# Matmuls of 256 columns in place of one of 512 in most k steps, and operand tiles at multiples of 2048 bytes

## The chip, the cores and the metric

The kernel runs on one core of one Trainium2 chip. The metric is the device time of one execution in microseconds (us); lower is better. A core has a matrix engine (PE, whose weight loads the profile lists apart as PEld), a vector engine (DVE), a scalar engine (ACT), GpSimd (POOL) and a sync engine (SP), which here issues nearly all transfers.

## The reference

One layer of an encoder trunk on 256 tokens with D = 2048, all in float32:

```python
u = rms_norm(h, norm_mix); proj = u @ w_in                      # 2048 x 5200
h = h + concat(gated_deltanet(...), mla_attention(...)) @ w_out
h = h + memory_cross_attention(rms_norm(h, norm_xattn), mem_n, wq, wk, wv, wo)
h = h + conv_ffn(rms_norm(h, norm_ffn), w_up, conv_w, conv_b, w_down)   # D_FF = 5632
return rms_norm(h, norm_final)
```

Nearly all arithmetic is in the products of 256 tokens with w_in, w_out, the four matrices of the cross-attention, w_up and w_down.

## The kernel before

**Products in three parts.** Each float32 operand is split into a high part, rounded to the matrix engine's one-pass format (fp32r), and the rest. A product is the sum of three: high weight by high token, high weight by low token, low weight by high token. A token tile `x(k)` holds, for 128 of the features, 256 columns of high parts and behind them 256 of low parts: 512 columns, 2048 bytes in each partition.

**k steps and output blocks.** Weights stay in the array, tokens move. One output block is 128 output features by 256 tokens in a PSUM tile `psg` of 512 columns. It is summed over k steps of 128 input features: 16 for a 2048-wide input, 44 for w_down, 8 for half a block of w_out. `kstep` (line 115) does one step with two matmuls: `wh` against all 512 columns (line 122, high result in columns 0 to 255, low in 256 to 511), and `wl` against the 256 high columns (line 120). `turn_` makes every other step take `wl` first, so that two products of one width stand side by side. `halves` and `add_res` add the two halves of the PSUM tile when they take it out. `kstep3` (lines 125 to 127) does the same step as three matmuls of 256 columns, all into columns 0 to 255; it is used where the result has no second half to add: `q_block` (tiles `xq`), the `lath` products, the scores (`kh`, `qh`), the mix of values (`pTx`, `vh`) and the last block of w_down. `v_block` (lines 958 to 960) has the tokens as weights and moves 512 columns of `wh` or `wl`.

**Weights.** `load_w` brings 128 x 1024 float32 (eight k steps) into `raw` by SP's queue; `split_w` makes `wh` on ACT (line 102) and `wl` on DVE (line 103). All three have four buffers in `wpool`.

**Order on PE.** The matrix engine's order is the order in which the code is written. Up to the cross-attention a queue of k steps (`drawn`, `enqueue`) is drawn by `fill(n)` between the small matmuls of attention and delta rule, so that PE has work while ACT and DVE prepare those. After that the blocks simply follow each other; `rstd_col` and `rstd_row` put a few small matmuls for a norm between two of them.

**Where the tiles lie.** Pools are laid out one behind the other in the order in which the program opens them. A tile's place in a partition, as the program was built:

| tile | first byte | modulo 2048 |
|---|---|---|
| `raw`, `wh`, `wl` (4 buffers each, 4096 bytes) | 19776, 36160, 52544 | 1344 |
| `small` pool, 10432 bytes | 68928 | 1344 |
| token tiles `u`, `xq`, `fx`, `xo`, `mh`, `om`, `od`, `ga` (16384 bytes a half) | 79360 and every 16384 on | 1536 |
| `gb`, feed-forward | 161280 | 1536 |
| `kh`, `qh`, `pTx`, `vh` | 204288, 194048, 214528, 218624 | 1536 |

One k step's weights are 512 bytes of `wh` or `wl`, so they begin at 1344, 1856, 320 or 832 modulo 2048. A moving operand begins at 1536 (high, or all 512 columns) or 512 (low).

Of the kernel before, what the change touches and what calls it, by code (L numbers as in the profile page):

```python
# [9 lines left out]
F32 = mybir.dt.float32  # L10
# [11 lines left out]
P = 128  # L22
T = 256
# [47 lines left out]
def trunk(ctx, tc, a):  # L71
    nc = tc.nc
    V, S, PE = nc.vector, nc.scalar, nc.tensor

    const = ctx.enter_context(tc.tile_pool(name="const", bufs=1))
    wpool = ctx.enter_context(tc.tile_pool(name="wpool", bufs=4))
    small = ctx.enter_context(tc.tile_pool(name="small", bufs=2))
    abpool = ctx.enter_context(tc.tile_pool(name="abpool", bufs=4))
    pg = ctx.enter_context(tc.tile_pool(name="pg", bufs=3, space=PSUM))
    pa = ctx.enter_context(tc.tile_pool(name="pa", bufs=5, space=PSUM))  # L80
# [1 line left out]
    def psg():  # L82
        return pg.tile([P, 512], F32, name="psg", tag="psg")

    def psa(tag="a"):
        return pa.tile([P, 512], F32, name="ps" + tag, tag=tag, bufs=1 if tag == "c" else 2)
# [19 lines left out]
    def load_w(src, n=1024, pieces=1):  # L106
        raw = wpool.tile([P, 1024], F32, name="raw", tag="raw")
        nc.sync.dma_start(raw[:, 0:n], src)
        return split_w(raw, n, pieces)

    turn_ = [False]

    def kstep(ps, wh, wl, xh2, first, last):
        rev = turn_[0] and not first
        turn_[0] = not rev
        for lo in ((True, False) if rev else (False, True)):
            if lo:
                PE.matmul(ps[:, 0:256], wl, xh2[:, 0:256], start=False, stop=last, skip_group_check=True)  # L120
            else:
                PE.matmul(ps[:, 0:512], wh, xh2, start=first, stop=last, skip_group_check=True)  # L122

    def kstep3(ps, wh, wl, xh2, first, last):
        PE.matmul(ps[:, 0:T], wh, xh2[:, 0:T], start=first, stop=False)  # L125
# [3 lines left out]
    def gemm_block(w, nb, x, step=kstep):  # L129
        ps = psg()  # L130
        for hf in range(2):
            wh, wl = load_w(w[2 * nb + hf])
            for j in range(8):
                k = 8 * hf + j
                step(ps, wh[:, j * P:(j + 1) * P], wl[:, j * P:(j + 1) * P], x(k), k == 0, k == KC - 1)
        return ps
# [22 lines left out]

    cg = const.tile([P, NCG], F32, name="cg")  # L160
    sm = const.tile([P, NSM], F32, name="sm")
    eps = const.tile([P, 1], F32, name="eps")
    epq = const.tile([P, 1], F32, name="epq")
    ones = cg[:, K_ONE:K_ONE + P]
# [1 line left out]


    def rstd_col(*accs):
        ps = psa("c")
        for t in range(2):  # L170
            for i, acc in enumerate(accs):
                PE.matmul(ps[:, t:t + 1], acc[:, t * P:(t + 1) * P], ones[:, 0:1], start=i == 0,
                          stop=i == len(accs) - 1)
        r = small.tile([P, 2], F32, name="rcol", tag="rcol", bufs=2)
        S.activation(r, ps[:, 0:2], AF.Sqrt, scale=1.0 / D, bias=eps)
        V.reciprocal(r, r)
        return r

    def rstd_row(col):
        ps = psa("c")  # L180
        for t in range(2):
            PE.matmul(ps[:, t * P:(t + 1) * P], col[:, t:t + 1].to_broadcast([P, P]), idn, start=True, stop=True)
        r = small.tile([P, T], F32, name="rrow", tag="rstd", bufs=2)
        S.copy(r, ps[:, 0:T])
        return r
# [4 lines left out]
    with ExitStack() as ph:  # L190
# [11 lines left out]
        with tc.tile_pool(name="xpool", bufs=1) as xpl:  # L202
# [13 lines left out]
            for k in range(KC):  # L216
                wh, wl = w0[k // 8]
                j = k % 8
                kstep(ps0, wh[:, j * P:(j + 1) * P], wl[:, j * P:(j + 1) * P], u(k), k == 0, k == KC - 1)
# [49 lines left out]
        def drawn():  # L269
            ready = {0: lead}  # L270
            ps = None
            i = 0
            while i < len(queue):
                for n in range(i, min(i + 1 + ahead[0], len(queue))):
                    if n not in ready:
                        ready[n] = load_w(queue[n][0], pieces=2)
                _, x, begin, first, last, done = queue[i]
                if begin:
                    begin()
                wh, wl = ready.pop(i)  # L280
                if first:
                    ps = psg()
                for j in range(8):
                    kstep(ps, wh[:, j * P:(j + 1) * P], wl[:, j * P:(j + 1) * P], x(j),
                          first and j == 0, last and j == 7)
                    if last and j == 7:
                        done(ps)
                    pos[0] += 1
                    for at_, f in [t for t in later if t[0] <= pos[0]]:
                        later.remove((at_, f))  # L290
                        f()
                    yield
                i += 1
# [3 lines left out]
        gen = drawn()  # L297

        def fill(n):
            for _ in range(n):  # L300
                next(gen, None)

        def until(n):
            fill(n - pos[0])
# [66 lines left out]
        with ExitStack() as ms:  # L371
# [20 lines left out]

            lats.append(latent)
            fill(8)
            rs0 = rstd_col(*accs)
            fill(6)
            rs.append(rstd_row(rs0))
            latent(0, ps0)
            latent(1, ps1)
            until(Q0 + 8)  # L400
            ps = psa()
# [72 lines left out]
            ps = psa()  # L474
# [5 lines left out]
            ps = psa()  # L480
# [22 lines left out]
            def w_mla(i):  # L503
                c = order.index(i)
                for n in order[c:c + 2]:
                    if n not in wm:
                        wm[n] = load_w(a["w_mla"][n])
                return wm[i]
# [63 lines left out]
            for i in range(2):  # L572
                kn = mp.tile([P, 4, T], F32, name="kn", tag="kn")
                wh, wl = w_mla(i)
                for n in range(4):
                    ps = psg()
# [8 lines left out]
                wh, wl = w_mla(2 + i)  # L585
                for t in range(2):
                    ps = psg()
# [325 lines left out]
    with ExitStack() as ph:  # L913
# [4 lines left out]
        for n in range(KC):  # L918
            wh, wl = load_w(a["w_out"][2 * n + 1])
            ps = psg()  # L920
# [15 lines left out]
        for n in range(KC):  # L936
            ps = gemm_block(a["xa_wk"], n, mh)
            if n == 0:
                rmc = rstd_col(macc)
                psk = ps  # L940
            else:
                if n == 1:
                    rsm = rstd_row(rmc)
                    normed(psk, rsm, kT[:, 0])
                normed(ps, rsm, kT[:, n])
            split_gain(xq(n), hT[:, n], sm[:, C_XA + n:C_XA + n + 1])
            accum_sq(xacc, hT[:, n], n == 0)
# [80 lines left out]
        for n in range(3):  # L1028
            v_block(n)
            if n == 0:  # L1030
                rcx = rstd_col(xacc)
            elif n == 1:
                rsx = rstd_row(rcx)
# [23 lines left out]
        for n in range(KC):  # L1057
            if n < 3:
                ps = pw[n]
            else:  # L1060
                ps = psg()
# [10 lines left out]
    with ExitStack() as ph:  # L1072
# [39 lines left out]
        for n in range(KC):  # L1112
            ps = psg()
            for c in range(6):
                nk = 8 if c < 5 else 4
                o = n * NF * P + c * 1024
                wh, wl = load_w(a["w_down"][n, :, c * 1024:c * 1024 + nk * P], nk * P)
# [131 lines left out]
```

## Time and profile before

| | |
|---|---|
| three runs, median | 1580.1 us (1579.47 to 1580.53) |
| profiled execution | 1580.7 us |
| its span, first to last instruction | 1578.9 us |
| mean granted PE clock | 0.994 |
| PE busy | 1546.1 us, 98% |
| DVE, ACT, POOL busy | 1119.3, 889.3, 147.9 us |
| moved by DMA | 282.22 MB, 179 GB/s |

Starts of matmuls are recorded, their ends are modelled; so the pace of PE is read from the distance between two starts, and not from the duration of one. A busy share of 98% says that PE had a matmul under way, not that its columns came at full rate.

### The profile page before, as it was taken

How to read it: one execution, taken by the hardware profiler on the slowest of the kernel's cores; microseconds unless marked ns; L12 is line 12 of the kernel's file. 1: busy time of each engine (PE TensorE's matmuls, PEld its weight loads, DVE VectorE, ACT ScalarE, POOL GpSimd, SP SyncE). 2: the span in 40 equal slices, each digit the busy share in tenths (PEclk: the TensorE clock that was granted, in tenths of full speed). 3: DMA queues.
4: the chain of work that ended last, by engine and by line, in shares of the span. 5: the costliest groups of instructions: out<-in, count | busy, mean ns of one | idle time of the engine just before them, and what ended most of it. 6: DMA issues, size and time to landing. Idle time of an engine off the chain costs nothing.

```text
span 1578.9 us, 24577 instructions
## 1 busy us (share of the span) xinstructions
PE 1546.1 (98%) x9386; PEld 1358.5 (86%) x9386; DVE 1119.3 (71%) x1810; ACT 889.3 (56%) x1473; POOL 147.9 (9%) x152
## 2 busy tenths in 40 slices
PE   7999999999999999999999999999999999999996
PEld 5887877888888889999888888888888888888886
DVE  8687688696976555566777888878888886445453
ACT  7867666757764444455556666556665665344441
POOL 2224021001320000000110000000000000111112
PEclk9999999999999999999999999999999999999998
DMA  7564443364665555544555555555555556666663
GB/s 248 179 214 141 144 134 126 118 214 132 200 200 189 191 188 193 174 161 133 174 188 187 187 189 190 194 188 189 192 193 187 187 190 183 190 190 183 198 187 106
DMA packets 80773, 282.22 MB, mean 179 GB/s; under 512 B 9392, under 2 KB 10304, under 8 KB 80656
## 3 DMA queue, kind: packets, MB, share of 16 engines
q1 hardware_dynamic: 79344, 277.86, 54.3%
q0 software_dynamic: 1312, 2.80, 0.6%
q8 instruction: 73, 1.20, 0.3%
q14 instruction: 44, 0.36, 0.1%
HBM read 277.83 MB, written 2.11 MB: 177 GB/s over the span
## 4 chain that ended last, share of the span: by engine, by line
PE 88%; DVE 5%; ACT 4%; issue 1%; DMA 1%; SPq 0%; DVEq 0%; ACTq 0%
PE psg L122 46%; PE psg L120 23%; PE psg L125 3%; PE psg L126 3%; PE psg L127 3%; PE psg L960 2%; PE psg L959 2%; PE psg L958 2%; DVE wl L103 2%; ACT wh L102 1%; DMA raw<-in_w_out_dram 1%; PE psa L620 0%; PE psa L539 0%; DVE qkv L330 0%; DVE hT L1132 0%
## 5 line engine op out<-in xcount | busy, mean ns | idle before, releaser
L103 DVE TENSOR_TENSOR wl<-raw,wh 128x1024 fp32r<-128x1024 f32 (+2 forms) x614 | 647.3, 1061 | 286.1 <-ACT wh L102 279.2
L102 ACT CAST wh<-raw 128x1024 fp32r<-128x1024 f32 (+2 forms) x614 | 550.8, 909 | 401.5 <-PE psg L122 243.2
L122 PE MATMUL psg<-fx,wh 128*128 128x512 f32 x1408 | 439.8, 393 | 0.0
L120 PEld LDWEIGHTS psg<-fx,wl 128*128 128x128 f32 x1408 | 264.7, 188 | 60.0
L120 PE MATMUL psg<-fx,wl 128*128 128x256 f32 x1408 | 277.6, 279 | 0.0
L122 PE MATMUL psg<-u,wh 128*128 128x512 f32 x624 | 207.7, 404 | 8.9 <-DVE u L149 8.2
L122 PEld LDWEIGHTS psg<-fx,wh 128*128 128x128 f32 x1408 | 212.0, 188 | 0.0
L120 PEld LDWEIGHTS psg<-u,wl 128*128 128x128 f32 x624 | 119.3, 192 | 29.3 <-DVE wl L103 3.1
L140 ACT COPY half<-psg 128x256 f32<-128x256 f32 x143 | 53.2, 372 | 154.9 <-PE psg L122 154.7
L120 PE MATMUL psg<-u,wl 128*128 128x256 f32 x624 | 134.3, 289 | 1.7 <-DVE wl L103 1.7
L122 PE MATMUL psg<-gb,wh 128*128 128x512 f32 x420 | 133.4, 393 | 0.0
L122 PEld LDWEIGHTS psg<-u,wh 128*128 128x128 f32 x624 | 99.3, 191 | 12.5 <-DVE u L149 9.0
L120 PEld LDWEIGHTS psg<-gb,wl 128*128 128x128 f32 x420 | 79.0, 188 | 17.9
L1089 DVE SCALAR_TENSOR_TENSOR y<-ub,sm,y 128x256 f32<-128x256 f32 x176 | 84.7, 482 | 3.5 <-ACT y L1087 0.3
L120 PE MATMUL psg<-gb,wl 128*128 128x256 f32 x420 | 82.8, 278 | 0.0
L122 PE MATMUL psg<-mh,wh 128*128 128x512 f32 x256 | 80.5, 394 | 0.0
L122 PE MATMUL psg<-xo,wh 128*128 128x512 f32 x256 | 80.4, 393 | 0.0
L141 DVE TENSOR_TENSOR ub<-psg,half 128x256 f32<-128x256 f32 x88 | 37.4, 425 | 60.1 <-ACT half L140 60.1
L122 PE MATMUL psg<-ga,wh 128*128 128x512 f32 x240 | 77.3, 393 | 0.0
L125 PE MATMUL psg<-xq,wh 128*128 128x256 f32 x256 | 71.2, 278 | 0.0
L126 PE MATMUL psg<-xq,wh 128*128 128x256 f32 x256 | 70.9, 277 | 0.0
L127 PE MATMUL psg<-xq,wl 128*128 128x256 f32 x256 | 70.9, 277 | 0.0
(405 smaller groups left out, 2411.3 us busy)
## 6 DMA issues: line engine op xcount, KB each, us to landing
raw<-in_w_up_dram SPq DMA_DIRECT2D x176, 512.0 KB, 3.4
raw<-in_w_down_dram SPq DMA_DIRECT2D x80, 512.0 KB, 4.2
raw<-in_w_in_dram SPq DMA_DIRECT2D x77, 512.0 KB, 3.9
raw<-in_w_out_dram SPq DMA_DIRECT2D x32, 512.0 KB, 4.2
raw<-in_xa_wk_dram SPq DMA_DIRECT2D x32, 512.0 KB, 3.5
raw<-in_xa_wv_dram SPq DMA_DIRECT2D x32, 512.0 KB, 3.5
raw<-in_xa_wq_dram SPq DMA_DIRECT2D x32, 512.0 KB, 3.4
raw<-in_xa_wo_dram SPq DMA_DIRECT2D x32, 512.0 KB, 3.4
```

Source lines behind the costliest of these rows:

```text
L102: S.copy(wh[:, c], raw[:, c])
L103: V.tensor_sub(wl[:, c], raw[:, c], wh[:, c].bitcast(F32))
L120: PE.matmul(ps[:, 0:256], wl, xh2[:, 0:256], start=False, stop=last, skip_group_check=True)
L122: PE.matmul(ps[:, 0:512], wh, xh2, start=first, stop=last, skip_group_check=True)
L125: PE.matmul(ps[:, 0:T], wh, xh2[:, 0:T], start=first, stop=False)
L126: PE.matmul(ps[:, 0:T], wh, xh2[:, T:2 * T], start=False, stop=False)
L127: PE.matmul(ps[:, 0:T], wl, xh2[:, 0:T], start=False, stop=last)
L140: S.copy(t, ps[:, T:2 * T])
L141: V.tensor_add(out, ps[:, 0:T], t)
L958: PE.matmul(pss[t], xh, wh[:, wk], start=(k == 0), stop=False)
L959: PE.matmul(pss[t], xh, wl[:, wk], start=False, stop=False)
L1089: V.scalar_tensor_tensor(y, b[:, j:j + T], sm[:, cw + j:cw + j + 1], y, ALU.mult, ALU.add)
```

## The change

`kstep` takes one of two forms. If it is the first step of an output block, or if the flag `wide` is set, the high weights meet all 512 columns as before. In every other step the high weights meet the high and the low 256 columns in two matmuls, both into columns 0 to 255, and the low weights follow always; the order no longer turns. The flag is set at each call of `fill`, `rstd_col` and `rstd_row`, and cleared by every step. The pool `small` is opened ahead of `wpool`, and a constant of 512 bytes that nothing reads is put in: `wpool` then begins at 30720, the token tiles at 79872, `gb` at 161792, and each of these is a multiple of 2048. All other tiles behind them move by 512 bytes.

```diff
     const = ctx.enter_context(tc.tile_pool(name="const", bufs=1))
+    small = ctx.enter_context(tc.tile_pool(name="small", bufs=2))
     wpool = ctx.enter_context(tc.tile_pool(name="wpool", bufs=4))
-    small = ctx.enter_context(tc.tile_pool(name="small", bufs=2))
...
-    turn_ = [False]
+    wide = [True]
 
     def kstep(ps, wh, wl, xh2, first, last):
-        rev = turn_[0] and not first
-        turn_[0] = not rev
-        for lo in ((True, False) if rev else (False, True)):
-            if lo:
-                PE.matmul(ps[:, 0:256], wl, xh2[:, 0:256], start=False, stop=last, skip_group_check=True)
-            else:
-                PE.matmul(ps[:, 0:512], wh, xh2, start=first, stop=last, skip_group_check=True)
+        if first or wide[0]:
+            PE.matmul(ps[:, 0:512], wh, xh2, start=first, stop=last, skip_group_check=True)
+        else:
+            PE.matmul(ps[:, 0:T], wh, xh2[:, 0:T], start=False, stop=False, skip_group_check=True)
+            PE.matmul(ps[:, 0:T], wh, xh2[:, T:2 * T], start=False, stop=False, skip_group_check=True)
+        wide[0] = False
+        PE.matmul(ps[:, 0:T], wl, xh2[:, 0:T], start=False, stop=last, skip_group_check=True)
...
+    const.tile([P, 128], F32, name="pad")
...
     def rstd_col(*accs):
+        wide[0] = True
...
     def rstd_row(col):
+        wide[0] = True
...
         def fill(n):
+            wide[0] = True
             for _ in range(n):
                 next(gen, None)
```

## Rows read from the trace of the kernel before

**Rows 1.** The page: the engines' busy time, and granted clock in 40 slices.

```profile
PE 1546.1 (98%) x9386; PEld 1358.5 (86%) x9386; DVE 1119.3 (71%) x1810; ACT 889.3 (56%) x1473; POOL 147.9 (9%) x152
PEclk9999999999999999999999999999999999999998
```

**Rows 2.** Windows: stretch, length, busy time of each engine, granted clock, DMA share, GB/s.

```profile
0.00:100.00 100.00, 87.65 (x482) 74.59 (x483) 78.82 (x156) 75.57 (x156) 23.45 (x31) 0.98 0.64 215
200.00:300.00 100.00, 94.06 (x637) 80.11 (x636) 76.76 (x175) 65.17 (x143) 13.98 (x9) 0.97 0.37 124
1000.00:1100.00 100.00, 100.00 (x579) 87.68 (x578) 81.49 (x127) 60.33 (x91) 0.00 (x0) 1.00 0.57 190
```

**Rows 3.** Groups of PE instructions: the matmuls of line 122, count, busy and mean.

```profile
L122 PE MATMUL psg<-fx,wh 128*128 128x512 f32 x1408 | 439.8, 393 | 0.0
...
L122 PE MATMUL psg<-u,wh 128*128 128x512 f32 x624 | 207.7, 404 | 8.9 <-DVE u L149 8.2 <-ACT wh L102 0.6
...
L122 PE MATMUL psg<-gb,wh 128*128 128x512 f32 x420 | 133.4, 393 | 0.0
...
L122 PE MATMUL psg<-mh,wh 128*128 128x512 f32 x256 | 80.5, 394 | 0.0
L122 PE MATMUL psg<-xo,wh 128*128 128x512 f32 x256 | 80.4, 393 | 0.0
L122 PE MATMUL psg<-ga,wh 128*128 128x512 f32 x240 | 77.3, 393 | 0.0
...
L122 PE MATMUL psg<-om,wh 128*128 128x512 f32 x128 | 41.9, 398 | 0.0
L122 PE MATMUL psg<-od,wh 128*128 128x512 f32 x128 | 40.2, 394 | 0.4 <-DVE hT L875 0.4
```

**Rows 4.** Timeline of PE in w_up: start us, us, engine, line, tiles, shape, count.

```profile
1000.31 0.39 PE L120 MATMUL psg<-fx,wl 128*128 128x256 f32 x2
1000.54 0.62 PE L122 MATMUL psg<-fx,wh 128*128 128x512 f32 x2
...
1011.40 0.39 PE L120 MATMUL psg<-fx,wl 128*128 128x256 f32 x2
```

**Rows 5.** Timeline of PE and its weight loads in `q_block`.

```profile
607.46 0.28 PE L125 MATMUL psg<-xq,wh 128*128 128x256 f32 x1
607.57 0.28 PE L126 MATMUL psg<-xq,wh 128*128 128x256 f32 x1
607.58 0.19 PEld L127 LDWEIGHTS psg<-xq,wl 128*128 128x128 f32 x1
...
612.56 0.28 PE L125 MATMUL psg<-xq,wh 128*128 128x256 f32 x1
```

**Rows 6.** Timeline of PE: into and out of the last block of w_down.

```profile
1548.96 0.39 PE L122 MATMUL psg<-gb,wh 128*128 128x512 f32 x1
1549.19 0.28 PE L125 MATMUL psg<-ga,wh 128*128 128x256 f32 x1
...
1564.74 0.28 PE L172 MATMUL psc<-cg,oacc 128*128 128x1 f32 x2
```

**Rows 7.** Timeline of PE: from `v_block` into the scores and out of them.

```profile
650.28 0.39 PE L960 MATMUL psg<-wh,mh 128*128 128x512 f32 x1
...
650.63 0.28 PE L126 MATMUL psa<-kh,qh 128*128 128x256 f32 x1
...
653.27 0.28 PE L127 MATMUL psa<-kh,qh 128*128 128x256 f32 x1
653.39 0.28 PE L125 MATMUL psg<-xq,wh 128*128 128x256 f32 x1
```

**Rows 8.** Timeline of PE: from `q_block` into the mix of values.

```profile
675.71 0.28 PE L127 MATMUL psg<-xq,wl 128*128 128x256 f32 x1
...
675.94 0.28 PE L126 MATMUL psa<-pTx,vh 128*128 128x256 f32 x1
...
677.62 0.28 PE L125 MATMUL psa<-pTx,vh 128*128 128x256 f32 x1
```

**Rows 9.** Timeline of PE: `q_block` interrupted by four transposes.

```profile
659.05 0.60 PE L1007 MATMUL psc<-cg,sx 128*128 128x128 f32 x4
...
659.84 0.28 PE L125 MATMUL psg<-xq,wh 128*128 128x256 f32 x1
...
660.52 0.28 PE L125 MATMUL psg<-xq,wh 128*128 128x256 f32 x1
```

## Prediction

> **What bounds the kernel now.** I read the page's busy times first, then the windows, the groups of PE, and last the timeline of PE, start by start. PE is busy for 98% of the span and at its full clock in nearly every slice [rows 1]. The windows say where it is not: it idles 12.4 us in the first 100 us and 5.9 us between 200 and 300 us; in a stretch of w_up it never stops, while DVE has 18% and the DMA engines 43% to spare [rows 2]. So from about 400 us on only one thing can change the time: how far apart the starts of successive matmuls are.
>
> The unit to count in is the k step. `kstep` runs 3460 times, the sum of the eight groups of line 122 [rows 3]. In w_up, 16 pairs of steps lie between 1000.31 and 1011.40 us: 11.09 us by 32 steps is 346.6 ns a step [rows 4]. At 2.4 GHz, the upper of PE's two clock levels and the one granted here (1.00), its 768 columns would pass in 320 ns.
>
> The timeline also shows what three matmuls of 256 columns cost, and that is the surprise of this trace: they have three prices, although columns, shape and granted clock are the same.
>
> - In `q_block`, 15 steps from 607.46 to 612.56 us: 340.0 ns a step, 113.3 ns a matmul [rows 5].
> - In the last block of w_down, 44 steps from 1549.19 to 1564.74 us: 353.4 ns a step, 117.8 ns a matmul [rows 6].
> - In the scores, 22 matmuls from 650.63 to 653.27 us, and in the mix of values, 14 from 675.94 to 677.62 us: 120.0 ns each, so 360.0 ns a step [rows 7, 8].
>
> The present step stands in the middle of the three. The sign of the change is therefore the question which price the new steps get.
>
> **What sets the price.** Waiting does not: these stretches run without a gap. The weight load of the next matmul starts 0.01 us after the matmul itself [rows 5], so a load of weights and a stream of tokens read SBUF side by side all the time, and both are nearly as long as the distance of two starts. Two things differ between the streams.
>
> One is where the two operands lie. In `q_block` and the last block, weights begin at 1344 plus a multiple of 512 and tokens at 1536 or 512: 320 apart modulo 512. In the scores and in the mix both begin at 1536 plus multiples of 512: 0 apart. Every stream with distance 0 runs at 120.0 ns, whatever went before: a 512-column stream in the scores [rows 7], the quick 113.3 ns stream in the mix [rows 8]. It takes the slow price from its second matmul on. I take the distance as the cause, though these streams also have their PSUM tiles from another pool, which I can't separate.
>
> The other is history. At distance 320 the same `q_block` code runs at 113.3 or at 117.8 ns: after an interruption by four transposes two steps take 0.68 us, the quick price [rows 9]; behind the 512-column matmul of `kstep` at 1548.96 us the slow price stays for the 132 matmuls that follow [rows 6].
>
> **The change part by part.**
>
> *The wide steps.* 206 steps open an output block: 2 for the first two of w_in, 53 in the queue (5 latent, 24 for q, k and v, 8 for z, 16 half blocks of w_out), and 16, 16, 16, 88 and 15 behind it. The calls of `fill`, `rstd_col` and `rstd_row` make some 80 more wide. These 286 keep one matmul of 512 columns and one of 256; only their order and addresses change. Bounds: 340.0 ns (three times 113.3) to 360.0 ns (three times 120.0), against 346.6 now: -1.9 to +3.8 us. I take 0.
>
> *The narrow steps.* 3460 less 286 are 3174. Each loses a matmul of 512 columns and gains two of 256, with a weight load each; columns are unchanged. Cost against 346.6 ns: -6.6 at the quick price, +6.8 at the middle one, +13.4 at the slow one; by 3174, -20.9, +21.6 or +42.5 us.
>
> *The alignment.* It makes weights begin at multiples of 512 and tokens at multiples of 1024 (modulo 2048): the distance becomes 0, as in the scores and the mix. So I take the slow price, +42.5 us. It also reaches code that the first edit doesn't touch. `q_block` has 256 steps that mostly run at 340.0 ns now: at 360.0, up to +5.1 us. The `lath` products (64 steps) and the last block (44) lie between 340 and 353 ns: +0.7 to +2.2 us. I take +5 for all of these. `v_block`'s 384 matmuls of 512 columns lie at distance 192 today, and no stream of that width at distance 0 is shown; from 650.28 to 650.63 us one of them and one matmul of 0.12 us start [rows 7], so one takes about 230 ns now; twice 113.3 and twice 120.0 ns bound it: -1.3 to +3.8 us. I take 0.
>
> *What costs nothing.* 3174 more matmuls and weight loads have to be fetched and issued; `q_block` already issues at that density without a gap [rows 5]. `wh` and `wl` are made by DVE and ACT at the pace at which PE uses them up; slower PE leaves them more room, a PE faster by 2% would raise DVE's 81% in w_up to 83% [rows 2]. The tiles behind the pad move by 512 bytes all together, and the distances among DVE's and ACT's operands in `wpool` stay the same. The bytes moved don't change, no semaphore is added, and PSUM tiles are opened and emptied as before.
>
> *What is hidden.* The 752 steps on `u` and `om` [rows 3], some 620 of them narrow, fall before 400 us, where PE waits for DVE and ACT at times [rows 2]. Their +8 us can in part fill those waits. I take 2 us off; bounds 0 and 8.
>
> **Sum.** 42.5 + 5 - 2 = +45.5 us. The profiled execution took 1580.7 us, its span 1578.9 and 1.8 us around it; the median of the runs is 1580.1, 0.6 us less. 1580.7 + 45.5 gives 1626 us, 2.9% slower. What a measurement can tell from no change is about 0.2%, 3 us.
>
> A rule of the Trainium skill speaks against the whole argument. Its page "SBUF — State Buffer", section "Who interferes with whom", gives the matrix engine two independent read ports, one for moving data and one for weights, and says that it never waits on anyone; then no address would matter, alignment would cost 0 and the narrow steps +21.6 or -20.9 us by history alone. The three prices of one instruction [rows 5 to 7] show that something beside columns and clock counts, but not yet what.
>
> **The rivals.**
>
> *Quick narrow steps (faster).* The wide step may leave the stream in the state in which `q_block` runs at 113.3 ns. A 512-column matmul is longer than a weight load, so the next weights are ready when it ends; and alignment may be just what makes that state last. For it: `q_block` holds the quick price over whole blocks [rows 5], and an interruption is enough to get there [rows 9]. Against it: at distance 320 a wide `kstep` left the slow price behind [rows 6], and at distance 0 no stream ran quick. It decides on the first narrow matmuls of a block; below 346.6 ns a step the change gains. Time: 1580.7 - 20.9, less or more 4 us of early steps that wait for others anyway: about 1560 us, 1555 to 1566.
>
> *History alone (slower, but less).* Addresses don't matter, and the narrow steps run as in the last block of w_down: 353.4 ns. For it: just this succession, one wide `kstep` and then narrow steps, is in the trace [rows 6]. Against it: the 120.0 ns streams [rows 7, 8]. Time: 1580.7 + 21.6 = 1602 us.
>
> *Columns alone (no change).* A step has 768 columns before and after, and blocks may mix quick and slow stretches so that they cancel. For it: all three prices lie within 4% of 346.6 ns. Against it: each of them holds over whole stretches. Time: 1580.7 us. The skill's page "TensorE: Matmul & The Clock Gate", section "Back-to-back issue gap", gives 2.5 ns to each matmul beside its columns; by that figure, an estimate, the change would cost 3174 by 2.5 ns, +7.9 us. The trace doesn't agree with 2.5 ns: here 256 columns take 6.6 to 13.3 ns more than the 106.7 they need.
>
> **How the numbers follow.** The slow price by distance 0 gets 0.42: every row at distance 0 is on its side, but none of them follows a wide step at distance 0. History alone gets 0.13, quick steps 0.37, columns alone 0.08. Slower is then 0.55, faster 0.37, same 0.08. The forecast's own range is 1600 to 1634: its lower end is about that of history alone, its upper end has the upper bounds of the narrow steps, of the streams that alignment alone reaches and of `v_block`, 42.5 + 7.3 + 3.8 us, and nothing hidden. As faster holds 0.37, the range that should hold 8 in 10 has to reach it: 1556 to 1634 us.
>
> **What would show it.** In the timeline of w_up the narrow steps stand 360 ns apart by the forecast, 353 by history, 340 if quick. The window from 1000 to 1100 us would hold about 833 matmuls (300 for 36 us), 849 or 882, against 579 now. `q_block` is the test of the alignment by itself, since only its addresses change: 120.0 ns throughout if distance decides, a mix of 113.3 and 117.8 ns if not. A `q_block` at 113.3 ns throughout, or narrow steps of w_up at 340 ns, would prove the forecast's central step wrong.

## The result, and the profile after

The changed kernel takes 1620.4 us (1619.96 to 1620.82, four runs) against 1580.2: a ratio of 1.0255, 95% interval 1.0237 to 1.0273. It is 40.2 us slower; 45.5 were forecast. The page of the kernel after, the counterpart of [rows 1]:

```profile
PE 1591.2 (98%) x12560; PEld 1544.2 (95%) x12560; DVE 1117.8 (69%) x1810; ACT 874.9 (54%) x1473; POOL 136.6 (8%) x152
PEclk9999999999999999999999999999999999999998
```

PE has 3174 matmuls and as many weight loads more, as counted beforehand, and is busy for 98% again, at its full clock. DVE has the same number of instructions and nearly the same time (1119.3 us before). So nothing new waits; the pace of PE changed. Its windows in the kernel after, as [rows 2]:

```profile
0.00:100.00 100.00, 89.51 (x666) 86.12 (x666) 78.37 (x154) 76.01 (x155) 24.95 (x31) 1.00 0.64 215
200.00:300.00 100.00, 96.77 (x786) 89.73 (x785) 79.71 (x180) 63.70 (x143) 13.17 (x9) 0.98 0.40 129
1000.00:1100.00 100.00, 100.00 (x818) 99.16 (x818) 77.86 (x123) 55.67 (x88) 0.00 (x0) 1.00 0.56 183
```

Look at the last row: 818 matmuls in 100 us, no gap, and DVE and ACT have less to do per microsecond than before, because PE uses weights up more slowly. The timeline of PE in the kernel after shows one output block of w_up there (columns as in [rows 4]):

```profile
1006.16 0.40 PE L118 MATMUL psg<-fx,wh 128*128 128x512 f32 x1
1006.40 0.28 PE L123 MATMUL psg<-fx,wl 128*128 128x256 f32 x1
1006.52 0.28 PE L120 MATMUL psg<-fx,wh 128*128 128x256 f32 x1
1006.64 0.28 PE L121 MATMUL psg<-fx,wh 128*128 128x256 f32 x1
1006.76 0.28 PE L123 MATMUL psg<-fx,wl 128*128 128x256 f32 x1
...
1011.91 0.40 PE L118 MATMUL psg<-fx,wh 128*128 128x512 f32 x1
```

One wide matmul takes 240 ns; the 46 of 256 columns behind it take 5.51 us, 119.8 ns each. That is the slow price of [rows 7, 8], now in the main stream. `q_block`, whose instructions the change didn't touch, in the timeline of the kernel after:

```profile
617.73 0.28 PE L126 MATMUL psg<-xq,wh 128*128 128x256 f32 x1
...
623.97 0.28 PE L127 MATMUL psg<-xq,wh 128*128 128x256 f32 x1
```

52 matmuls in 6.24 us: 120.0 ns, where [rows 5] had 113.3.

Two views by tile say how much of that lies where (duration min/median/max, then the first and the last start in us). Before, tiles `om` and `fx`:

```profile
L122 PE MATMUL psg<-om,wh x128: 388/396/501, 340.7 to 405.0; 128*128 128x512 f32 x128
L122 PE MATMUL psg<-fx,wh x1408: 388/394/483, 831.4 to 1320.2; 128*128 128x512 f32 x176
```

After:

```profile
L123 PE MATMUL psg<-om,wl x128: 274/283/287, 342.5 to 407.1; 128*128 128x256 f32 x128
L123 PE MATMUL psg<-fx,wl x1408: 279/283/287, 844.4 to 1351.2; 128*128 128x256 f32 x176
L118 PE MATMUL psg<-fx,wh x88: 396/403/476, 844.2 to 1345.6; 128*128 128x512 f32 x88
```

The stream on `om` ends only 2 us later than before. w_up takes 507.0 us instead of 488.8, 18.2 us more.

### The profile page after: what moved, and what is told of

Read it like the earlier page. It is cut to its first block, busy times and chain, and to the rows that moved or that the text cites. A ratio compares the mean times of both kernels' runs of the same rounds, so it can differ in the third digit from the quotient of the medians.

```text
span 1618.7 us, 31093 instructions
## 1 busy us (share of the span) xinstructions
PE 1591.2 (98%) x12560; PEld 1544.2 (95%) x12560; DVE 1117.8 (69%) x1810; ACT 874.9 (54%) x1473; POOL 136.6 (8%) x152
## 4 chain that ended last, share of the span: by engine, by line
PE 91%; DVE 4%; ACT 3%; DMA 1%; issue 1%; SPq 0%; DVEq 0%; ACTq 0%
PE psg L123 24%; PE psg L120 22%; PE psg L121 22%; PE psg L118 4%; PE psg L128 3%; PE psg L126 3%; PE psg L127 3%; PE psg L963 2%; PE psg L964 2%; PE psg L965 2%; DVE wl L103 2%; ACT wh L102 1%; PE psa L625 1%; DMA raw<-in_w_out_dram 1%; PE psa L544 0%
## 5 line engine op out<-in xcount | busy, mean ns | idle before, releaser
L123 PE MATMUL psg<-fx,wl 128*128 128x256 f32 x1408 | 398.4, 283 | 0.0
L121 PE MATMUL psg<-fx,wh 128*128 128x256 f32 x1320 | 373.7, 283 | 0.0
L120 PE MATMUL psg<-fx,wh 128*128 128x256 f32 x1320 | 373.6, 283 | 0.0
L120 PEld LDWEIGHTS psg<-fx,wh 128*128 128x128 f32 x1320 | 250.9, 190 | 4.1
L121 PEld LDWEIGHTS psg<-fx,wh 128*128 128x128 f32 x1320 | 251.0, 190 | 0.0
L123 PE MATMUL psg<-u,wl 128*128 128x256 f32 x624 | 178.7, 286 | 1.0 <-DVE wl L103 1.0
L120 PE MATMUL psg<-u,wh 128*128 128x256 f32 x517 | 149.6, 289 | 1.2 <-ACT wh L102 0.7
L121 PE MATMUL psg<-u,wh 128*128 128x256 f32 x517 | 148.5, 287 | 0.0
L123 PE MATMUL psg<-gb,wl 128*128 128x256 f32 x420 | 118.9, 283 | 0.0
L121 PE MATMUL psg<-gb,wh 128*128 128x256 f32 x420 | 118.9, 283 | 0.0
L120 PE MATMUL psg<-gb,wh 128*128 128x256 f32 x420 | 118.9, 283 | 0.0
L120 PEld LDWEIGHTS psg<-u,wh 128*128 128x128 f32 x517 | 100.1, 194 | 6.8 <-ACT wh L102 1.0
L121 PEld LDWEIGHTS psg<-u,wh 128*128 128x128 f32 x517 | 100.3, 194 | 0.8 <-issue 0.5
L121 PEld LDWEIGHTS psg<-gb,wh 128*128 128x128 f32 x420 | 80.0, 190 | 0.0
L120 PEld LDWEIGHTS psg<-gb,wh 128*128 128x128 f32 x420 | 80.0, 190 | 0.0
L126 PE MATMUL psg<-xq,wh 128*128 128x256 f32 x256 | 72.7, 284 | 0.0
```

The costliest lines, as they stand in the source:

```text
L120: PE.matmul(ps[:, 0:T], wh, xh2[:, 0:T], start=False, stop=False, skip_group_check=True)
L121: PE.matmul(ps[:, 0:T], wh, xh2[:, T:2 * T], start=False, stop=False, skip_group_check=True)
L123: PE.matmul(ps[:, 0:T], wl, xh2[:, 0:T], start=False, stop=last, skip_group_check=True)
```

## The experiments

**How they are read.** All experiments change the k step, the addresses, or both. For the addresses two numbers are enough: by how much the high weights and by how much the low weights begin past the moving operand, modulo 256. They are written H/L: 64/64 before, 0/0 after. (The prediction counted modulo 512; why 256 is right is the third experiment.) Means of the distance between two starts are taken over all such matmuls of a stream in the trace, with addresses from the program as built. "Narrow step" means the new form of `kstep` with its wide steps. The theories: distance sets the price (the forecast), history alone sets it, or the wide matmul does.

**1. The alignment alone** (the k step of before, pools and pad of after):

```diff
     const = ctx.enter_context(tc.tile_pool(name="const", bufs=1))
+    small = ctx.enter_context(tc.tile_pool(name="small", bufs=2))
     wpool = ctx.enter_context(tc.tile_pool(name="wpool", bufs=4))
-    small = ctx.enter_context(tc.tile_pool(name="small", bufs=2))
...
+    const.tile([P, 128], F32, name="pad")
```

> Alignment alone, with the k step of before (one matmul of 512 columns and one of 256, order turning). If the distance between weights and tokens modulo 512 sets the price: q_block, untouched in its code, goes from 340 to 360 ns a step, and the turning k step gets dearer too, about as the wide steps of the changed kernel (234 to 241 and 117 to 120 ns), some 355 ns against 346.6, so 1600 to 1615 us. If the form of the narrow step sets the price: q_block stays at 340 ns and the time within 5 us of 1580.

1590.5 us, ratio 1.0068 (1.0048 to 1.0088). The same `q_block` code in its timeline:

```profile
614.83 0.28 PE L125 MATMUL psg<-xq,wh 128*128 128x256 f32 x1
...
616.99 0.28 PE L125 MATMUL psg<-xq,wh 128*128 128x256 f32 x1
```

18 matmuls in 2.16 us: 120.0 ns, and over all of `q_block` the mean is 120 too. The instructions, their order and their PSUM pool are those of before; only addresses differ. So the distance is a cause by itself, and the PSUM pool, which the prediction could not separate, is not needed for it. The turning step hardly minds the address: 348.4 ns against 346.7 in w_up. My expectation of its cost was too high.

**2. The narrow steps alone** (the k step of after, the layout of before, 64/64):

```diff
-    turn_ = [False]
+    wide = [True]
...
+        if first or wide[0]:
+            PE.matmul(ps[:, 0:512], wh, xh2, start=first, stop=last, skip_group_check=True)
+        else:
+            PE.matmul(ps[:, 0:T], wh, xh2[:, 0:T], start=False, stop=False, skip_group_check=True)
+            PE.matmul(ps[:, 0:T], wh, xh2[:, T:2 * T], start=False, stop=False, skip_group_check=True)
...
```

> The narrow steps alone, tiles where they lay before (distance 320). If the distance sets the price: no stream of narrow steps in psg at 360 ns a step; 353.4 (1602 us) if the wide first step leaves the middle price behind, 340 (1560 us) if it leaves the quick one. If three matmuls into the same columns cost 120 ns each by their form: 360 ns a step and 1620 us as with the change.

1599.8 us, ratio 1.0135 (1.0119 to 1.0150). A block of w_up in its timeline:

```profile
1006.19 0.28 PE L123 MATMUL psg<-fx,wl 128*128 128x256 f32 x1
...
1011.61 0.40 PE L118 MATMUL psg<-fx,wh 128*128 128x512 f32 x1
```

46 matmuls in 5.42 us: 117.8 ns, the middle price of [rows 6], 353.1 ns a step over all of w_up. Only two of its 88 blocks run otherwise: the second and the third, each behind four small matmuls for a norm, at 113.6 and 113.4 ns. +20.6 us alone and +11.3 us for the alignment alone make 31.9; together they cost 40.2, 8 more (11 by the profiled spans: 39.8 less 10.6 and 17.8). The reason is in the steps: the alignment costs a narrow one 6.7 ns (359.8 against 353.1) and a turning one 1.7; for the 2557 narrow steps behind `om` the difference makes 12.8 us.

**3 and 4. Several distances in one kernel.** Weight tiles of 1040 instead of 1024 elements lie 4160 bytes apart, so the four buffers have four distances. First in the kernel after without its pad (modulo 512, H: 0, 64, 128, 192; L: 256 more), then in the layout of before with tokens moved by 64 bytes (H: 256, 320, 384, 448; L: 256 less):

```diff
-        wh = wpool.tile([P, 1024], F32R, name="wh", tag="wh")
-        wl = wpool.tile([P, 1024], F32R, name="wl", tag="wl")
+        wh = wpool.tile([P, 1040], F32R, name="wh", tag="wh")
+        wl = wpool.tile([P, 1040], F32R, name="wl", tag="wl")
```

> The changed kernel with the weight buffers 4160 instead of 4096 bytes apart: the four buffers of wh lie 0, 64, 128 and 192 bytes from the tokens modulo 512, those of wl 256, 320, 384 and 448. If only distance 0 is dear: the runs of eight steps on buffer 0 keep 120 ns a matmul, those on the others fall to 113 to 118 ns, and the time is 1570 to 1605 us. If every multiple of 64 is the same to the chip: 120 ns on all four and 1620 us. If a shorter period than 512 counts, two or more of the four buffers are at 120 ns.

> As the kernel with the buffers 4160 bytes apart, but with the tokens moved so that the four buffers of wh lie 256, 320, 384 and 448 bytes from them modulo 512 and those of wl 0, 64, 128 and 192. If only distance 0 is dear: the first and last product of each step at 113 to 118 ns on all four buffers, the middle one, under which wl is loaded, at 120 ns on the first buffer alone; 1560 to 1600 us. If a period of 256 counts: 120 ns on the first buffer throughout. If distance does nothing: 1620 us.

One run each, 1608.3 and 1605.2 us. In the timeline of the first, weights at H 64 and then, in the next block, at H 0:

```profile
1004.32 0.28 PE L120 MATMUL psg<-fx,wh 128*128 128x256 f32 x1
...
1006.44 0.28 PE L120 MATMUL psg<-fx,wh 128*128 128x256 f32 x1
...
1010.33 0.28 PE L120 MATMUL psg<-fx,wh 128*128 128x256 f32 x1
...
1011.77 0.28 PE L120 MATMUL psg<-fx,wh 128*128 128x256 f32 x1
```

18 matmuls in 2.12 us are 117.8 ns each, 12 in 1.44 us are 120.0, in one stream and of one line. In that 120.0 ns buffer the low weights lie 256 from the tokens; in the second kernel the high ones do, and its first buffer runs at 120.0 as well, here 14 matmuls in 1.68 us:

```profile
1007.98 0.28 PE L122 MATMUL psg<-fx,wh 128*128 128x256 f32 x1
...
1009.66 0.28 PE L125 MATMUL psg<-fx,wl 128*128 128x256 f32 x1
```

All other buffers of both run at 117.5 to 118.7 ns. Buffer by buffer the two kernels agree within 0.1 ns a step (359.0, 355.0, 353.6 and 352.3 in the median), although in the second all of these tiles lie 64 bytes further modulo 256 and every distance is another one modulo 512. So it is the distance that counts and not the address itself, and the period is 256: 0 and 256 are alike, and 64, 128 and 192 are nearly alike as long as H and L agree modulo 256.

**5. No wide matmul in any k step** (64/64; everything is summed into columns 0 to 255, one copy takes it out):

```diff
+        PE.matmul(ps[:, 0:T], wh, xh2[:, 0:T], start=first, stop=False, skip_group_check=True)
+        PE.matmul(ps[:, 0:T], wh, xh2[:, T:2 * T], start=False, stop=False, skip_group_check=True)
         PE.matmul(ps[:, 0:T], wl, xh2[:, 0:T], start=False, stop=last, skip_group_check=True)
```

> No matmul of 512 columns in any k step, tiles where they lay before (distance 320); a product has one half only, so the second half is neither taken out nor added. If it is the wide step that puts the narrow ones behind it into the 117.8 ns price, and small matmuls for the norms put them into the 113.3 ns one: long stretches at 340 ns a step and 1555 to 1570 us. If the quick price is peculiar to q_block: 353 ns a step and about 1600 us.

1601.9 us, ratio 1.0149 (1.0132 to 1.0166), and 353.3 ns a step in w_up. The wide matmul is not what keeps that stream at the middle price; that theory fell. In the early streams on `u` and `om`, which wait now and then, and in `q_block` 113 to 114 ns occur often, as in [rows 9]. The first blocks of w_up show a switch:

```profile
847.52 0.50 PE L164 MATMUL psc<-cg,facc 128*128 128x1 f32 x4
...
848.31 0.28 PE L114 MATMUL psg<-fx,wh 128*128 128x256 f32 x1
...
853.30 0.28 PE L116 MATMUL psg<-fx,wl 128*128 128x256 f32 x1
853.42 0.60 PE L174 MATMUL psc<-cg,rcol 128*128 128x128 f32 x4
...
854.10 0.28 PE L116 MATMUL psg<-fx,wl 128*128 128x256 f32 x1
```

Ahead of 847.52 us the stream runs at 117.8 ns. Between the two interruptions 44 matmuls pass in 4.99 us, 113.4 ns each; behind the second it runs at 117.8 again. So four small matmuls can switch this stream either way, and without one the price stays for the rest of w_up.

**6 and 7. The turning step at other distances.** The k step of before with tiles 4160 bytes apart (H = L = 64, 128, 192, 0), and with 1028 elements, which take 4128 bytes (H/L 64/192, 96/224, 128/0, 160/32):

```diff
+        wh = wpool.tile([P, 1028], F32R, name="wh", tag="wh")
+        wl = wpool.tile([P, 1028], F32R, name="wl", tag="wl")
```

> The kernel before with weight buffers 4160 bytes apart; modulo 256 the distances of its four buffers of wh are 64, 128, 192 and 0. If distance sets the price of the turning step too: 346.6 ns a step on the first buffer as before, 348 on the last as with the alignment alone, and something else on the two between, 340 to 350 ns. If distance matters to narrow steps alone: 346.6 on all. The time stays within 8 us of 1580 either way; the starts tell.

> The kernel before with weight buffers 4128 bytes apart; modulo 256 the distances are 64, 96, 128 and 160 for wh and 192, 224, 0 and 32 for wl. If lines of 64 bytes are what collides, the odd multiples of 32 are dearer than 64 (a weight slice or a token row then begins inside a line): over 350 ns a step on two of four buffers. If only 0 modulo 256 is special: 346 to 348 ns on all.

One run each, 1587.2 and 1591.7 us: 9 and 14 us above the 1578.0 of before beside them. The buffers of the first take 345.8 to 350.3 ns a step. In the second, 64/192 and 96/224 take 347.5, 160/32 350.5 and 128/0 351.1, so it is not the odd multiples of 32 that are dear, as the expectation had it. The wide matmul takes 228.3 ns with H at 64 in the second and 230 to 233 elsewhere. No buffer gives the turning step a gain worth the name.

**8. The narrow step with 4128 bytes.** The narrow runs so far had kept H and L equal modulo 256. Here they differ by 128:

> One wide step and narrow ones as in the change, tiles as before but weight buffers 4128 bytes apart; distances modulo 256 as in the turning kernel with 4128 bytes. If some distance lets the quick price survive the wide step: 113 to 115 ns a matmul on one buffer and under 1590 us. If history alone decides outside distance 0: 117 to 119 ns on all and 1598 to 1605 us.

One run, 1602.6 us. By the sum it shows nothing; by buffer it shows the way. 64/192 has means of 115.2, 114.7 and 115.4 ns for the three matmuls of a step, with medians of 113 to 114; the three others stay at 116.7 to 121.1. At 128/0, where the low weights alone lie at distance 0, the means are 118.1, 116.7 and 118.2 ns: one of the two at 0 doesn't make the stream slow. The timeline enters that buffer at 1007.03 us and settles after some matmuls:

```profile
1007.03 0.28 PE L120 MATMUL psg<-fx,wh 128*128 128x256 f32 x1
1007.16 0.28 PE L121 MATMUL psg<-fx,wh 128*128 128x256 f32 x1
...
1007.98 0.28 PE L123 MATMUL psg<-fx,wl 128*128 128x256 f32 x1
...
1009.68 0.28 PE L123 MATMUL psg<-fx,wl 128*128 128x256 f32 x1
1009.80 0.39 PE L118 MATMUL psg<-fx,wh 128*128 128x512 f32 x1
```

From 1007.98 to 1009.68 us 15 matmuls pass, 113.3 ns each.

**9 to 12. 64/192 for all buffers.** A tile of 128 bytes that nothing uses is put between the `wh` and the `wl` buffers and another behind `wl`, so that the tokens stay at 0:

```diff
+    pads = {"a": 0, "b": 128, "c": 128}
+
+    def pad(g):
+        if pads[g]:
+            wpool.tile([P, pads[g] // 4], F32, name="pad" + g, tag="pad" + g, bufs=1)
+            pads[g] = 0
...
         wh = wpool.tile([P, 1024], F32R, name="wh", tag="wh")
+        pad("b")
         wl = wpool.tile([P, 1024], F32R, name="wl", tag="wl")
+        pad("c")
```

Four kernels: the narrow step with it, the turning step with it, no wide matmul with it, and as a control the narrow step with the distances exchanged (192/64, pads ahead of `raw` and between `wh` and `wl`).

> The narrow k step in the old layout, with 128 bytes between the high and the low weight tiles, so that every high tile lies 64 bytes and every low tile 192 bytes past a multiple of 256, and the tokens stay at 0. Theory A (the pair of distances sets the price, also without a change of distance from buffer to buffer): the w_up stream runs at what the one buffer with 64 and 192 showed in the run with 4128 bytes between buffers, 115.2, 114.7 and 115.4 ns, 345.3 ns a step against 353.1 in the narrow step alone: 3174 x 7.8 = 25 us less than 1599.8, 1575 us; if the medians of 113 to 114 hold throughout, 340 ns and 1558 us. Rival B (that buffer was quick because its neighbours lay at other distances): 117.8 ns and 1600 us.

> The k step of before with the same 128 bytes between high and low tiles. Theory A: the distance also sets what the turning step pays: with high tiles at 64 the wide matmul took 228.3 ns in the run of 4128 bytes against 230 to 233 elsewhere, the low one 117 to 119, 345.8 ns a step against 346.7: 1577 us, same within 0.3%. Rival B (the low tile's distance acts on the 256-column matmul after a wide one as it does on narrow ones): 114 instead of 116 ns, 343 ns a step, 1568 us. Rival C (nothing moves): 1580 us.

> No 512-column matmul in any k step, sums in one half, the same 128 bytes between high and low tiles. Theory A with the wide step's price left out: as the narrow step with these distances, and nothing more: 1558 to 1577 us. Rival B (a wide step once a block keeps the narrow ones behind it from 113.3 ns): 340 ns a step and 1556 us here while the other narrow version stays at 1575 us or more.

> The control: the narrow k step with the two distances exchanged, high tiles 192 bytes and low tiles 64 bytes past a multiple of 256. Theory A1 (it matters that the two differ by 128): as with 64 and 192, 1558 to 1577 us. Theory A2 (it matters which of the two lies at 64): 117.8 ns and 1600 us. Rival B (neighbouring buffers at other distances made it quick): 1600 us.

The narrow step at 64/192 takes 1563.9 us, ratio 0.9898 (0.9884 to 0.9913): faster than both kernels. Its timeline in w_up, across the border of two blocks:

```profile
1006.15 0.28 PE L131 MATMUL psg<-fx,wh 128*128 128x256 f32 x1
...
1007.86 0.39 PE L129 MATMUL psg<-fx,wh 128*128 128x512 f32 x1
1008.08 0.28 PE L134 MATMUL psg<-fx,wl 128*128 128x256 f32 x1
1008.20 0.28 PE L131 MATMUL psg<-fx,wh 128*128 128x256 f32 x1
1008.32 0.28 PE L132 MATMUL psg<-fx,wh 128*128 128x256 f32 x1
1008.44 0.28 PE L134 MATMUL psg<-fx,wl 128*128 128x256 f32 x1
1008.55 0.28 PE L131 MATMUL psg<-fx,wh 128*128 128x256 f32 x1
...
1012.98 0.28 PE L131 MATMUL psg<-fx,wh 128*128 128x256 f32 x1
```

Ahead of the wide matmul 15 take 1.71 us, 114 ns each. Behind it the first four stand 0.12 us apart; then 39 take 4.43 us, 113.6 ns each. Here a wide matmul does disturb the stream, but only for a few starts. From the window 1000 to 1100 us, one row of each: the narrow, the turning, the one without wide matmuls, and the control.

```profile
1000.00:1100.00 100.00, 100.00 (x864) 99.33 (x863) 81.80 (x129) 59.08 (x92) 0.00 (x0) 1.00 0.57 195
```

```profile
1000.00:1100.00 100.00, 100.00 (x579) 88.59 (x578) 81.54 (x127) 60.30 (x91) 0.00 (x0) 1.00 0.55 190
```

```profile
1000.00:1100.00 100.00, 100.00 (x885) 100.00 (x884) 73.68 (x113) 59.75 (x92) 0.00 (x0) 1.00 0.56 194
```

```profile
1000.00:1100.00 100.00, 100.00 (x845) 99.25 (x845) 80.22 (x126) 57.23 (x90) 0.00 (x0) 1.00 0.55 190
```

The turning step stays at its 579 matmuls: 1578.1 us, ratio 0.9990 (0.9980 to 0.9999). Its two parts do move, as they did with H at 64 in experiment 7: the wide matmul takes 227.6 ns instead of 231.0 and the low one 119.2 instead of 115.8, and the two cancel. Without wide matmuls w_up runs at 340.2 ns a step, the quick price throughout, but the whole takes 1566.5 us, ratio 0.9913 (0.9896 to 0.9929): its stream on `om` starts its last matmul at 412.2 us, against 403.8 with wide steps. In that early part PE idles 27.2 us instead of 19.6, and of this it waits 7.8 us for ACT's `pT` instead of 1.2; why, no run shows. The control takes 1588.5 us, ratio 1.0056 (1.0041 to 1.0071); in its timeline 24 matmuls ahead of a wide one pass in 2.72 us, 113.3 ns each, and behind it they stand about 119 ns apart:

```profile
999.82 0.28 PE L131 MATMUL psg<-fx,wh 128*128 128x256 f32 x1
...
1002.54 0.39 PE L129 MATMUL psg<-fx,wh 128*128 128x512 f32 x1
...
1002.88 0.28 PE L131 MATMUL psg<-fx,wh 128*128 128x256 f32 x1
...
1005.97 0.28 PE L134 MATMUL psg<-fx,wl 128*128 128x256 f32 x1
```

From the third block of w_up to the last, slow and quick blocks alternate, 118.8 and 113.6 ns in the mean. They also alternate between two pairs of weight buffers, but the first block runs at 113.6 on the pair that is slow later, so the buffers alone don't decide it. At 192/64 a stretch can thus be quick or not, by what went before, while at 64/192 every block of w_up is quick (113.8 to 114.2); that H and L differ by 128 is not enough by itself. Of the expectations, theory A held for the narrow step: 341.4 ns a step, near the better of its two prices. The kernel without wide matmuls lies in its range too; for the turning step the time can't tell theory A (1577 us) from no change. For the control neither of its two forms holds; it lies between them.

All kernels with wide steps and one distance for every buffer, in one table; the step is the mean in w_up, of the narrow steps alone where there are some. The runs of before beside these had medians of 1579.2 to 1580.2 us:

| k step | H/L | ns a step | us |
|---|---|---|---|
| turning (before) | 64/64 | 346.7 | 1580.2 |
| turning, aligned | 0/0 | 348.4 | 1590.5 |
| turning | 64/192 | 346.8 | 1578.1 |
| narrow, aligned (after) | 0/0 | 359.8 | 1620.4 |
| narrow | 64/64 | 353.1 | 1599.8 |
| narrow | 192/64 | 348.4 | 1588.5 |
| narrow | 64/192 | 341.4 | 1563.9 |

## Why the prediction was right

*The count and the bound.* The 3174 narrow steps are there [rows 3], PE stays the only bound, and no wait was added.

*The narrow steps, +42.5 us.* The price taken, 360.0 ns, is the one that came: 359.8 in w_up, 360 in w_down and the cross-attention. w_up alone was to grow by 1320 by 13.4 ns, 17.7 us, and grew by 18.2 with its 88 wide steps.

*Distance as the cause.* It was taken from streams that also had another PSUM pool. The alignment alone (1) separated them: distance 0 does it. The prediction also read weight loads as nearly as long as the distance of two starts; in [rows 5] a load is recorded with 0.19 us and two starts lie 0.113 us apart, so one load laps over the next. That they run beside the matmuls, all that the argument needed, holds. The step was right in substance and wrong in its period: not modulo 512 but 256 (3, 4). Since 320 is 64 and 0 is 0 by either, this changed no number.

*History as the other factor.* At 64/64 the narrow step alone gave 353.1 ns, as forecast for that rival; +20.6 us against its +21.6. But the wide `kstep` in front is not the reason (5). At 64/64 some streams run quick and others don't. Small matmuls in between can switch them (5); what they set in the chip stays open.

*The alignment on other code, +5 us.* `q_block` at 120.0 ns throughout, the test named beforehand. It went from 343.8 to 360.9 ns a step in the mean, 4.4 us; `v_block`, taken as 0, got 0.8 us shorter. The aligned kernel (1) fits: 3460 by 1.7 ns are 5.9 us and `q_block` again some 4; 11.3 were measured.

*The wide steps, 0 (-1.9 to +3.8).* In w_up the wide matmul takes 238.8 ns and the low one 119: 358 ns against 346.7, and for 286 that would be +3.2 us where nothing hides it. At the upper bound, not in the middle.

*What is hidden, -2 us (0 to 8).* This term was mis-sized. The early narrow steps cost 620 by 13.4 ns, 8.3 us, and `om` ends only 2 us later. The windows up to its last matmul, before and after:

```profile
0.00:405.00 405.00, 385.31 (x2442) 330.43 (x2442) 312.94 (x655) 282.51 (x602) 74.88 (x83) 0.99 0.50 164
0.00:407.10 407.10, 392.25 (x3059) 368.34 (x3060) 313.63 (x658) 282.04 (x604) 74.78 (x83) 1.00 0.50 164
```

PE idles 14.9 us there instead of 19.7: 4.8 us went into the waits. The granted clock gave up to 3 us more: 0.98 and 0.97 in the first two windows of [rows 2], 1.00 and 0.98 in the same windows after. The prediction had no term for the clock; whether the change raised it or chance did, no run shows. With 3174 by 13.1 ns, +3 for the wide steps, +5 and -8 for both of these the sum is about +42; 40.2 were measured. That the forecast lay within 6 us of the result is thus in part luck: the wide steps taken as 0 and the early part taken as too little err to opposite sides.

*The count of matmuls.* The window was said to show 833. That forgot the wide matmul of each block: 47 matmuls in 5.75 us make 817 in 100 us, and 818 are there. The narrow steps at 64/64 reach 833 by coincidence.

*The rivals.* Quick narrow steps were possible, and alignment is what ruled them out: to hold in every block they need 64/192 (9), not distance 0. Columns alone fell. The page "SBUF — State Buffer" of the Trainium skill, section "Who interferes with whom", would make the addresses free, since it gives moving data and weights independent read ports. The runs disagree: kernels 2 and 9 issue the same instructions and differ by two unused tiles of 128 bytes, and they lie 35.9 us apart. Which part of the chip makes the distance count no run here shows.

## What to carry to other kernels

Where a matrix engine at full clock never idles, read its pace from the starts, and look for one instruction that has several prices in the trace; here three prices of a 256-column matmul told what an edit of "the same columns" would cost. Splitting a wide matmul into two is neither good nor bad by itself: it went from +2.5% to -1.0% with the place of the weights relative to the tokens. Try a few paddings between the tiles of the two operands, several in one kernel if there are several buffers, and read the price buffer by buffer before judging the split; round addresses may be the worst ones.

## What the runs showed of the hardware

- A 256-column fp32r matmul with its own weight load starts 113.3 to 120.0 ns after the one before it, at full clock and without a wait, by the distance of weights and moving data modulo 256 bytes: 120.0 where high and low weights both lie at 0, 113.8 in the mean for 64/192, 116.1 for 192/64 (w_up, narrow steps). Where both lie at 64, 128 or 192 it was mostly 117.5 to 118.7.
- What went before counts as well: at 64/64 four small matmuls switched a stream from 117.8 to 113.4 ns, and the next four switched it back (5); at 192/64 blocks of 118.8 and 113.6 ns alternate.
- A matmul of 512 columns minds the distance too: behind narrow ones it takes 238.8 ns at 0/0, 227.8 at 64/192 (means in w_up).
- A stream with alternating 512 and 256 columns evens the distances out: 346.7 to 348.4 ns a step at 64/64, 0/0 and 64/192.
